# A hybrid decoder layer on one core: stores moved from SP to GpSimd, small copies to ScalarE, other token tiles, and fewer columns in two kinds of row

## The chip, the core and the metric

The kernel runs on one core of a Trainium2 chip. The core has TensorE (PE; its weight loads are shown apart as PEld), VectorE (DVE), ScalarE (ACT), GpSimd (POOL), the DMA queue of SyncE (SP), and 16 DMA engines that all queues share. Each engine takes its instructions in the order of its own list; semaphores tie the lists together. The metric is the device time of one execution in microseconds (us); less is better.

## What is computed

One layer of a decoder over 16 meta tokens, 1024 prompt tokens and 8 samples of 8 tokens (1104 tokens of width 1024). The reference, cut to what matters:

```
hn = rmsnorm(h, norm_mix_pre)
proj = hn @ w_in                      # 1024 -> 512 + 512 + 512 + 1024 + 1536 + 16
gate_b, gate_c, hv, z, xbc, dt_raw = split(proj)
u = gate_c * hv
conv_u, new_buf_sc = causal_dwconv(u, buf_sc, sconv_w)          # 3 taps
ya = group_rmsnorm(gate_b * conv_u, sconv_norm, 8)
xbc_c = silu(causal_dwconv(xbc, buf_xbc, ssm_conv_w) + ssm_conv_b)   # 4 taps
y, s = ssd_chunked(x, dt, A, B, C, s0)     # 16 meta tokens, 8 chunks of 128; samples from their own state
y = (y + D_skip * x) * silu(z)
yb = group_rmsnorm(y, ssm_norm, 2)
h = h + rmsnorm(concat(ya, yb) @ w_out, norm_mix_post)
fn = rmsnorm(h, norm_ffn_pre)
h = h + rmsnorm((silu(fn @ w_gate) * (fn @ w_up)) @ w_down, norm_ffn_post)
```

Returned are the outputs of the prompt and the samples (not of the meta tokens) and the new states: the last 2 rows of u, the last 3 rows of xbc, and the SSD state s.

## The kernel before

**Layout.** Channels lie on the partitions and tokens along the free dimension: a "row" is 128 channels of one projection by all 1104 tokens, in one of 5 buffers (`row_tile`). A row's tokens are in this order: 16 meta, 1024 prompt, 64 sample tokens. The tokens of one projection are cut into three tiles (`CUTS`): 272, 384 and 448 columns. The normalized input stands in SBUF once for each tile as a high and a low part (`xh`, `xl`); the weights of a row are split in the same way (`split_w`: a load `raw`, a copy `whi` on ACT, a subtraction `wlo` on DVE). `project_tile` makes one tile of one row: 8 blocks of the contraction by 3 products (high by high, low by high, high by low), 24 matmuls into one PSUM bank.

**Stages.** (1) Token tiles of x are loaded, normalized, transposed by PE (`split_x`) and split into `xh` and `xl`, while the first two xbc rows (8 and 9) and dt are projected. (2) The other xbc rows are projected, convolved (`taps`) and stored in DRAM (`d_xbc`). (3) The SSD's stretch: a loop over 8 chunks of 128 tokens (`ssd_chunk`, `y_of`), with the state updates of the samples (`sample_state`, 8 units) and the gating of finished chunks (`finish`) between. PE is filled there with the projections of z (`z_rows`, 8 rows) and of the short convolution (`sconv_gate` for c, `sconv_conv` for hv, called v, `sconv_out` for b, 4 rows each). (4) The output projection (`o`), (5) gate and up, (6) down.

**What passes through DRAM in stage 3.** `d_z` (z rows) and `d_y` (a chunk's y) are stored and loaded again by `finish`, as `zt` and `yf`; `finish` stores `d_yb`, and `sconv_out` stores `d_ya`, which stage 4 loads as `mrb` and `mra`. `sample_state` loads a state `s` (one of 2 buffers) and stores its successor to `o_nat`. A chunk loads its x, B and C (`xb`, 2 buffers), two tables of decays (`M`, 3 buffers; `E`, one), and has one buffer for y.

**Order.** The source gives instructions and priorities; a scheduler sets each engine's list when the program is built, from its own estimate of when operands and buffers are ready. A DMA stands in the list of the engine that issues it, here SP for all, and waits there until its data is ready or its buffer is free; what is behind it in that list waits too. Every DMA also waits until an earlier DMA that used its semaphore has landed; the semaphores of a queue are taken in turn, eight for SP and eight for GpSimd.

`sconv_conv` works like this: GpSimd clears the first 2 columns of u and copies the samples' history (`shist`) into u; the product of c and hv is written behind them, tile by tile; GpSimd copies u's last columns to `slast`, which leaves as the new state; ACT makes the last tap and DVE adds the others.

Of the kernel before, what the change touches and what calls it, by code (L numbers as in the profile page):

```python
# [27 lines left out]
DFF = 2816  # L28
NF = DFF // P
EPS = 1e-6  # L30
CUTS = [(0, 272), (272, 384), (656, 448)]
NT = 448
TT = [(0, NMETA)] + [(NMETA + P * i, P) for i in range(NCH)] + [(TS0, NS * LS)]
O_GB, O_GC, O_HV, O_Z, O_X, O_DT = 0, 512, 1024, 1536, 2560, 4096
ROW = 1152
HPF = 500
NACC = 2
YB = 1
SAMP = {1: (0,), 2: (1,), 3: (2, 3), 4: (4, 5), 5: (6,), 6: (7,)}
LATE = (9,)  # L40
WIDE = True
# [14 lines left out]
def hymba_kernel(ctx, tc, x_prompt, x_sample, state_sconv, state_ssm_conv, state_ssm, meta_tokens,  # L56
# [167 lines left out]
        for t in range(3):  # L224
            yield (t,) + project_tile(w_, t, name, skip=skip)

    def parts(t, pad):


        a, n = CUTS[t]  # L230
        b = a + n
        out = [(slice(0, min(b, TS0) - a), slice(pad + a, pad + min(b, TS0)))]
        if b > TS0:
            out.append((slice(TS0 - a, n), None))
        return out
# [65 lines left out]
    def split_x(i):  # L301

        xt, w = xts[i], P if i else MS
        pt = ps.tile([P, KD, P], F32, tag="big", name=f"xT{i}")
        for ks in (range(0, 4), range(4, 8)) if i < 3 else (range(KD),):
            for k in ks:
                PE.transpose(pt[:, k, :w], xt[:w, k * P:(k + 1) * P], ident[:w, :w])
            kk = slice(ks[0], ks[-1] + 1)
            for t0, c0, n in ((TT[i][0], 0, P),) if i else ((0, 0, NMETA), (TS0, NMETA, NS * LS)):
                t = max(q for q in range(3) if CUTS[q][0] <= t0)  # L310
                sl = slice(t0 - CUTS[t][0], t0 - CUTS[t][0] + n)
                dh, dl = xh[t][:, kk, sl], xl[t][:, kk, sl]
                S.activation(dh, pt[:, kk, c0:c0 + n], AF.Copy)
                V.tensor_tensor(out=dl, in0=pt[:, kk, c0:c0 + n], in1=dh.bitcast(F32), op=ALU.subtract)
# [205 lines left out]
    def y_of(i, xb, bt, xd, off):  # L520

        t0, w = TT[i]
        c = i - 1
        smp = i > NCH
        if smp:
            E = po.tile([P, 8, NS * LS], F32, tag="ES", name="ES")
            y = po.tile([P, 8, NS * LS], F32, tag="yS", name="yS")
        else:
            E = po.tile([P, 8, P], F32, tag="E", name=f"E{i}")
            y = po.tile([P, 8, P], F32, tag="y", name=f"y{i}", bufs=YB)  # L530
        for e in range(2):
            SY.dma_start(E[64 * e:64 * e + 64, :, :w],
                         d_e[:, c, :w].rearrange("(j e) t -> e j t", e=2)[e].partition_broadcast(64))
        pcb = ps.tile([P, 2, P], F32, tag="small", name=f"pcb{i}", bufs=NSM)
        cb = po.tile([P, 2, P], F32, tag="cb", name=f"cb{i}")
        mask = U if w == P else Us
        for g in range(2):
            PE.matmul(pcb[:w, g, :w], xb[:, 8 + g, :w], xb[:, 10 + g, :w], start=True, stop=True)
        V.tensor_tensor(out=cb[:w, :, :w], in0=pcb[:w, :, :w], in1=mask[:w, :w].unsqueeze(1).to_broadcast([w, 2, w]),
                        op=ALU.mult)  # L540
        Ms = []
        for g in range(2):
            M = m_tile(f"M{i}{g}")
            SY.dma_start(M[:w, :, :w], d_a[8 * g:8 * g + 8, c, :w].partition_broadcast(w))
            mg = M[:w, :, :w]
            for h in range(8):
                a_s = a_tok[:w, i, 8 * g + h:8 * g + h + 1]
                if g == 0:
                    V.tensor_scalar(out=M[:w, h, :w], in0=M[:w, h, :w], scalar1=a_s, scalar2=0.0,
                                    op0=ALU.subtract, op1=ALU.min)  # L550
                else:
                    S.activation(M[:w, h, :w], M[:w, h, :w], AF.Relu, scale=-1.0, bias=a_s)
            S.activation(mg, mg, AF.Exp, scale=1.0 if g == 0 else -1.0)
            V.tensor_tensor(out=mg, in0=mg, in1=cb[:w, g, :w].unsqueeze(1).to_broadcast([w, 8, w]), op=ALU.mult)
            Ms.append(M)
        if not smp:
            po_ = big(f"po{i}")
            pov = po_.rearrange("p (j t) -> p j t", j=8)
            off(pov)
        for j in range(8):  # L560
            S.activation(y[:, j, :w], xb[:, j, :w], AF.Copy, scale=Dp[:, j:j + 1])
        if not smp:
            V.tensor_tensor(out=E, in0=pov, in1=E, op=ALU.mult)
        pd_ = big(f"pd{i}")
        pdv = pd_.rearrange("p (j t) -> p j t", j=8)
        for h in range(H):
            e = h % 2
            PE.matmul(pdv[64 * e:64 * e + 64, h // 2, :w], xd[:w, h * 64:(h + 1) * 64], Ms[h // 8][:w, h % 8, :w],  # L568
                      start=True, stop=True)
        if not smp:  # L570
            V.tensor_tensor(out=y, in0=y, in1=E, op=ALU.add)
        V.tensor_tensor(out=y[:, :, :w], in0=pdv[:, :, :w], in1=y[:, :, :w], op=ALU.add)
        if smp:
            return E, y
        SY.dma_start(d_y[i][:, :, :], y)

    def finish(i):
        t0, w = TT[i]
        y = pf.tile([P, 8, P], F32, tag="yf", name=f"yf{i}", bufs=2)
        SY.dma_start(y[:, :, :w], d_y[i][:, :, :])  # L580
        zt = pf.tile([P, 8, P], F32, tag="zt", name=f"zt{i}")
        SY.dma_start(zt[:, :, :w], d_z[:, :, t0:t0 + w].rearrange("j p t -> p j t"))
        yv = y[:, :, :w]
        V.tensor_tensor(out=yv, in0=yv, in1=zt[:, :, :w], op=ALU.mult)
        sq = zt
        S.activation(sq[:, :, :w], yv, AF.Square)
        sg = pf.tile([P, 2, P], F32, tag="sg", name=f"sg{i}")
        sv = sq[:, :, :].rearrange("p (g j) t -> p g j t", g=2)[:, :, :, :w]
        V.tensor_tensor(out=sv[:, :, 0:2], in0=sv[:, :, 0:2], in1=sv[:, :, 2:4], op=ALU.add)
        V.tensor_tensor(out=sg[:, :, :w], in0=sv[:, :, 0], in1=sv[:, :, 1], op=ALU.add)  # L590
        pn = ps.tile([P, 2, P], F32, tag="small", name=f"pn{i}", bufs=NSM)
        PE.matmul(pn[:, :, :w], ones, sg[:, :, :w], start=True, stop=True)
        S.activation(sg[:, :, :w], pn[:, :, :w], AF.Sqrt, bias=eps_c, scale=0.25 / 512)
        V.reciprocal(sg[:, :, :w], sg[:, :, :w])
        for g in range(2):
            yg = y[:, 4 * g:4 * g + 4, :w]
            V.tensor_tensor(out=yg, in0=yg, in1=sg[:, g, :w].unsqueeze(1).to_broadcast([P, 4, w]), op=ALU.mult)
        SY.dma_start(d_yb[i][:, :, :], yv)

    def states(i, bt, xw):  # L600
        t0, w = TT[i]
# [15 lines left out]
    def z_rows():  # L617
        for j in range(8):
            row = row_tile(f"z{j}")
            for t, sl, pt in project(O_Z + j * P, f"pz{j}", NMETA):  # L620
                with tc.high_priority(offset=HPF):
                    S.activation(row[:, sl], pt, AF.Tanh, scale=0.5)
                    V.scalar_tensor_tensor(out=row[:, sl], in0=row[:, sl], scalar=1.0, in1=pt,  # L623
                                           op0=ALU.add, op1=ALU.mult)
            SY.dma_start(d_z[j][:, NMETA:T], row[:, NMETA:T])
            yield

    srow = {}

    def sconv_gate(j):  # L630
        gc = srow["gc", j] = row_tile(f"gc{j}")
        for t, sl, pt in project(O_GC + j * P, f"pc{j}"):
            with tc.high_priority(offset=HPF):
                S.activation(gc[:, sl], pt, AF.Copy)

    def sconv_conv(j):
        gc, u = srow["gc", j], row_tile(f"u{j}")
        smp = sample_rows(u, 2)
        G.memset(u[:, 0:2], 0.0)
        G.tensor_copy(smp[:, :, 0:2], shist[:, j, :].rearrange("p (b i) -> p b i", i=2))  # L640
        for t, sl, pt in project(O_HV + j * P, f"ph{j}"):
            for pc, rc in parts(t, 2):
                g_ = gc[:, sl.start + pc.start:sl.start + pc.stop]
                with tc.high_priority(offset=HPF):
                    if rc is not None:
                        V.tensor_tensor(out=u[:, rc], in0=pt[:, pc], in1=g_, op=ALU.mult)
                    else:
                        V.tensor_tensor(out=smp[:, :, 2:2 + LS], in0=b_i(pt[:, pc]), in1=b_i(g_), op=ALU.mult)
        G.tensor_copy(slast[:, j, 0:16].rearrange("p (b i) -> p b i", i=2), smp[:, :, LS:LS + 2])
        G.tensor_copy(slast[:, j, 16:18], u[:, TS0:TS0 + 2])  # L650
        wcol = lambda i: 60 + i * 4 + j
        taps(gc, u, 2, wcol, None, vec)
        taps(b_i(gc[:, TS0:T]), smp, 2, wcol, None, vec, None, lambda t, i: t[:, :, i:i + LS])

    def sconv_out(j):
        gc = srow["gc", j]
        for t, sl, pt in project(O_GB + j * P, f"pb{j}", NMETA):
# [10 lines left out]
            for h in (slice(0, n // 2), slice(n // 2, n)) if j == 3 else (slice(0, n),):  # L668
                V.reciprocal(sq[:, h], sq[:, h])
            V.tensor_tensor(out=gc[:, sl], in0=gc[:, sl], in1=sq, op=ALU.mult)  # L670
        SY.dma_start(d_ya[j][:, NMETA:T], gc[:, NMETA:T])

    def sconv_rows():
        for step in SORD.split():
# [49 lines left out]
    def sample_state(u, st):  # L724
# [38 lines left out]
        V.tensor_tensor(out=s0, in0=pt.rearrange("p (j n) -> p j n", j=8), in1=s0, op=ALU.add)  # L763
        for q in range(2):
            rows = slice((j0 + q) * P, (j0 + q + 1) * P)
            SY.dma_start(o_nat[b0:b0 + 4, rows, :].rearrange("b q n -> q b n"), s0[:, 4 * q:4 * q + 4, :])
        pv = ps.tile([P, 8, 3, LS], F32, tag="small", name=f"so{u}", bufs=NSM)
        for q in range(8):
            for n in range(3):
# [5 lines left out]
        V.tensor_tensor(out=t, in0=t, in1=E[:, j0:j0 + 2, tl], op=ALU.mult)  # L775
        V.tensor_tensor(out=y[:, j0:j0 + 2, tl], in0=y[:, j0:j0 + 2, tl], in1=t, op=ALU.add)
        if u == NS - 1:
            SY.dma_start(d_y[NCH + 1][:, :, :], y)

    def conv_states():  # L780
        for q in range(2):
# [3 lines left out]
            o = s_tile(f"xlo{q}")[0:27, :, :].rearrange("p j t -> p (j t)")[:, 0:6 * P]  # L785
            V.tensor_copy(o, pt[0:27, 0:6 * P])
            sl = slice(q * 6 * P, (q + 1) * 6 * P)
            SY.dma_start(o_xc_s[0].flatten_outer_dims()[:, sl], o[0:24, :])
            SY.dma_start(o_xc_p[0, 0][:, sl], o[24:27, :])

    def final_state():
        pt = big("fsp")
# [662 lines left out]
```

## Time and profile before

| what | us |
|---|---|
| three runs | 1412.11, 1418.18, 1409.39 |
| their median | 1412.11 |
| the profiled execution | 1411.28 |
| its span, first to last instruction | 1409.6 |

The profile is of one execution. Its page gives busy times of the engines, the chain of work that ended last, and the costliest groups of instructions; other views give the waits of each engine, busy times by stretch, and instructions in order of time. A row such as "L219 PE MATMUL px<-xh,whi" names the line, the engine, the operation, the tile written and the tiles read. SPq is SP's DMA queue. A matmul's duration contains its way through the array, and matmuls overlap: what one costs is the distance from its start to the next one's.

### The profile page before, as it was taken

The numbers are of one execution on the slowest core, as the hardware profiler recorded it, in microseconds if no ns is written. First come the engines' busy times: TensorE is split into PE (matmuls) and PEld (weight loads), VectorE is DVE, ScalarE is ACT, GpSimd is POOL, SyncE is SP. The second block draws the span as 40 slices with busy tenths as digits, with TensorE's granted clock in tenths as the row PEclk, the third lists the DMA queues.
The fourth block names the chain that finished last, engine by engine and source line by source line (L and its number), as shares of the span: only waits on it lengthen the run. The fifth ranks groups of instructions, "written<-read, shape, count | busy, mean of one in ns | idle before, by whom it ended". The sixth has DMA issues, their size and how long they took to land.

```text
span 1409.6 us, 22023 instructions
## 1 busy us (share of the span) xinstructions
PE 1374.2 (97%) x8841; PEld 1248.3 (89%) x8841; DVE 974.4 (69%) x1333; ACT 586.3 (42%) x946; POOL 50.7 (4%) x110
## 2 busy tenths in 40 slices
PE   7999999999999999999999999999999999999997
PEld 5899998788888987887889999999999998888886
DVE  6645457787797988687489877666767666455565
ACT  6456344444354344566554232222322334344431
POOL 1100000000000100011010000000000000000010
PEclk9999999999999999999999999999999999999999
DMA  6135246776746448775445553445343469655553
GB/s 212 47 88 168 81 117 192 199 207 196 203 136 191 133 135 282 243 228 179 146 140 181 189 195 116 162 163 174 133 140 107 160 218 324 228 179 165 180 161 129
DMA packets 212543, 240.51 MB, mean 171 GB/s; under 512 B 33421, under 2 KB 161505, under 8 KB 212442
## 3 DMA queue, kind: packets, MB, share of 16 engines
q1 hardware_dynamic: 212442, 239.12, 53.1%
q8 instruction: 69, 1.13, 0.3%
q14 instruction: 32, 0.26, 0.1%
HBM read 170.29 MB, written 68.79 MB: 170 GB/s over the span
## 4 chain that ended last, share of the span: by engine, by line
PE 79%; DVE 9%; DMA 7%; ACT 3%; issue 2%; SPq 0%; POOL 0%; DVEq 0%; POOLq 0%; ACTq 0%
PE d L1388 13%; PE px L219 10%; PE o L1004 9%; PE yg L1045 7%; PE yu L1045 7%; PE pz L219 5%; PE zg L1045 4%; PE zu L1045 4%; PE xu L1045 4%; PE xg L1045 4%; PE pb L219 2%; DMA M<-d_a 2%; PE pc L219 2%; DMA zt<-d_z 1%; PE pd L568 1%
## 5 line engine op out<-in xcount | busy, mean ns | idle before, releaser
L219 PE MATMUL px<-xh,whi 128*128 128x384 f32 (+2 forms) x288 | 94.1, 335 | 0.0
L219 PE MATMUL px<-xh,wlo 128*128 128x384 f32 (+2 forms) x288 | 92.7, 330 | 0.0
L219 PE MATMUL px<-xl,whi 128*128 128x448 f32 (+2 forms) x288 | 92.4, 331 | 0.0
L97 DVE TENSOR_TENSOR wlo<-raw,whi 128x1024 fp32r<-128x1024 f32 x32 | 39.1, 1222 | 55.8 <-ACT whi L105 55.7
L996 DVE SCALAR_TENSOR_TENSOR wol<-wo,vec,woh 128x1024 fp32r<-128x1024 f32 x36 | 45.9, 1278 | 30.7 <-ACT woh L995 30.7
L219 PE MATMUL pz<-xh,whi 128*128 128x256 f32 (+2 forms) x192 | 65.3, 340 | 1.1 <-DVE z L623 1.1
L219 PE MATMUL pz<-xl,whi 128*128 128x256 f32 (+2 forms) x192 | 63.4, 330 | 0.0
L219 PE MATMUL pz<-xh,wlo 128*128 128x256 f32 (+2 forms) x192 | 63.2, 329 | 0.0
L995 ACT ACTIVATE woh<-wo,vec 128x1024 fp32r<-128x1024 f32 x36 | 41.4, 1149 | 51.1 <-PE o L1004 42.0
L219 PEld LDWEIGHTS px<-xh,whi 128*128 128x128 f32 x288 | 53.8, 190 | 2.3 <-issue 0.2
L219 PEld LDWEIGHTS px<-xl,whi 128*128 128x128 f32 x288 | 53.1, 188 | 1.9
L219 PEld LDWEIGHTS px<-xh,wlo 128*128 128x128 f32 x288 | 53.3, 188 | 1.6
L1388 PE MATMUL d<-wd,B01h 128*128 128x512 f32 x176 | 54.2, 389 | 0.0
L249 DVE SCALAR_TENSOR_TENSOR xa<-xr,vec,xa 128x1128 f32<-128x1128 f32 x36 | 50.1, 1391 | 0.7
L1004 PE MATMUL o<-wol,mhb 128*128 128x512 f32 x144 | 44.5, 396 | 3.0 <-DVE wol L996 3.0
L1388 PE MATMUL d<-wd,T3h 128*128 128x512 f32 x152 | 46.8, 389 | 0.0
L1388 PE MATMUL d<-wd,T2h 128*128 128x512 f32 x144 | 44.2, 389 | 0.0
L1388 PE MATMUL d<-wd,B11h 128*128 128x512 f32 x144 | 44.2, 389 | 0.0
L276 ACT ACTIVATE xr<-px 128x384 f32<-128x384 f32 (+1 forms) x36 | 16.0, 457 | 58.5 <-PE px L219 58.4
L1004 PE MATMUL o<-woh,mlb 128*128 128x512 f32 x128 | 40.0, 391 | 0.0
L219 PEld LDWEIGHTS pz<-xh,whi 128*128 128x128 f32 x192 | 36.1, 188 | 4.2 <-issue 1.6
L105 ACT ACTIVATE whi<-raw 128x1024 fp32r<-128x1024 f32 x32 | 33.8, 1055 | 14.2 <-PE ph L219 8.9
(692 smaller groups left out, 4087.3 us busy)
## 6 DMA issues: line engine op xcount, KB each, us to landing
wo<-in_w_out_dram SPq DMA_DIRECT2D x36, 512.0 KB, 3.9
raw<-in_w_in_dram SPq DMA_DIRECT2D x32, 512.0 KB, 5.2
wg<-in_w_gate_dram SPq DMA_DIRECT2D x11, 1024.0 KB, 7.1
wu<-in_w_up_dram SPq DMA_DIRECT2D x11, 1024.0 KB, 5.2
xr<-in_w_down_dram SPq DMA_DIRECT2D x11, 1024.0 KB, 5.4
d_t<-xr SPq DMA_DIRECT2D x11, 1024.0 KB
xt<-in_x_prompt_dram SPq DMA_DIRECT2D x16, 512.0 KB, 6.4
M<-d_a SPq DMA_DIRECT2D x16, 512.0 KB, 5.1
```

The costliest lines, as they stand in the source:

```text
L97: V.tensor_tensor(out=out, in0=a, in1=hi.bitcast(F32), op=ALU.subtract)
L105: S.activation(hi[:, :], raw[:, :], AF.Copy)
L219: PE.matmul(acc, (hi, lo, hi)[q][:, wk], (xh, xh, xl)[q][t][:, k, o:], start=n_ == 0, stop=n_ + 1 == len(order))
L249: V.scalar_tensor_tensor(out=dst, in0=part(row, i), scalar=wv[:, wcol(i):wcol(i) + 1], in1=dst, op0=ALU.mult, op1=ALU.add)
L276: S.activation(row[:, rc], pt[:, pc], AF.Copy)
L568: PE.matmul(pdv[64 * e:64 * e + 64, h // 2, :w], xd[:w, h * 64:(h + 1) * 64], Ms[h // 8][:w, h % 8, :w], start=True, stop=True)
L995: S.activation(hi, raw, AF.Copy, scale=nv)
L996: V.scalar_tensor_tensor(out=lo, in0=raw, scalar=nv, in1=hi[:, :].bitcast(F32), op0=ALU.mult, op1=ALU.subtract)
L1004: PE.matmul(accs[i][c], l[:, kb, :], r_[:, c * 512:(c + 1) * 512], start=n == 0 and q == 0, stop=n == 11 and q == len(steps) - 1)
L1045: PE.matmul(acc[:, c, 0:W1], w_[l][k], b[r_][:, k, c * W1:(c + 1) * W1], start=start and k == 0 and x == 0, stop=k == 3 and x == 2, skip_g ...
L1388: PE.matmul(accs[t], sx[x][:, tl], wx[y], start=st and x + y == 0, stop=en and x == 1, skip_group_check=n not in OPENS)
```

## The change

Three things change.

Stores. In stage 3 the stores of z rows, of y (chunks and samples), of `d_yb` (chunks), of `d_ya`, of the samples' states, and of the last xbc rows (`conv_states`) are issued by GpSimd. The small copies of `sconv_conv` go from GpSimd to ACT.

Tiles. `CUTS` becomes 272, 320 and 512 columns. Token tile 5 (columns 528 to 655) now lies half in the second and half in the third tile, so `split_x` copies it in two parts.

Columns. The rows c and hv leave out the first 12 of the 16 meta tokens (`SKIP`), since their ya is never used; the taps of the prompt start at the first prompt token, so they read u from meta token 14 on, and the clearing of u's first columns goes away.

```
-CUTS = [(0, 272), (272, 384), (656, 448)]
-NT = 448
+CUTS = [(0, 272), (272, 320), (592, 512)]
+NT = 512
+SKIP = NMETA - 4
...
-    def parts(t, pad):
+    def parts(t, pad, skip=0):
...
+        a += skip if t == 0 else 0
+        n = b - a
...
-            for t0, c0, n in ((TT[i][0], 0, P),) if i else ((0, 0, NMETA), (TS0, NMETA, NS * LS)):
+            cut = [(TT[i][0], 0, P)] if i != 5 else [(TT[5][0], 0, P // 2), (TT[5][0] + P // 2, P // 2, P // 2)]
+            for t0, c0, n in cut if i else ((0, 0, NMETA), (TS0, NMETA, NS * LS)):
...
-        SY.dma_start(d_y[i][:, :, :], y)
+        G.dma_start(d_y[i][:, :, :], y)
...
-        SY.dma_start(d_yb[i][:, :, :], yv)
+        (G if w == P else SY).dma_start(d_yb[i][:, :, :], yv)
...
-            SY.dma_start(d_z[j][:, NMETA:T], row[:, NMETA:T])
+            G.dma_start(d_z[j][:, NMETA:T], row[:, NMETA:T])
...
-        for t, sl, pt in project(O_GC + j * P, f"pc{j}"):
+        for t, sl, pt in project(O_GC + j * P, f"pc{j}", SKIP):
...
-        G.memset(u[:, 0:2], 0.0)
-        G.tensor_copy(smp[:, :, 0:2], shist[:, j, :].rearrange("p (b i) -> p b i", i=2))
-        for t, sl, pt in project(O_HV + j * P, f"ph{j}"):
-            for pc, rc in parts(t, 2):
+        S.activation(smp[:, :, 0:2], shist[:, j, :].rearrange("p (b i) -> p b i", i=2), AF.Copy)
+        for t, sl, pt in project(O_HV + j * P, f"ph{j}", SKIP):
+            for pc, rc in parts(t, 2, SKIP):
...
-        G.tensor_copy(slast[:, j, 0:16].rearrange("p (b i) -> p b i", i=2), smp[:, :, LS:LS + 2])
-        G.tensor_copy(slast[:, j, 16:18], u[:, TS0:TS0 + 2])
+        S.activation(slast[:, j, 0:16].rearrange("p (b i) -> p b i", i=2), smp[:, :, LS:LS + 2], AF.Copy)
+        S.activation(slast[:, j, 16:18], u[:, TS0:TS0 + 2], AF.Copy)
...
-        taps(gc, u, 2, wcol, None, vec)
+        taps(gc[:, NMETA:TS0], u, 2, wcol, None, vec, None, lambda t, i: t[:, NMETA + i:TS0 + i])
...
-        SY.dma_start(d_ya[j][:, NMETA:T], gc[:, NMETA:T])
+        G.dma_start(d_ya[j][:, NMETA:T], gc[:, NMETA:T])
...
-            SY.dma_start(o_nat[b0:b0 + 4, rows, :].rearrange("b q n -> q b n"), s0[:, 4 * q:4 * q + 4, :])
+            G.dma_start(o_nat[b0:b0 + 4, rows, :].rearrange("b q n -> q b n"), s0[:, 4 * q:4 * q + 4, :])
...
-            SY.dma_start(d_y[NCH + 1][:, :, :], y)
+            G.dma_start(d_y[NCH + 1][:, :, :], y)
...
-            SY.dma_start(o_xc_s[0].flatten_outer_dims()[:, sl], o[0:24, :])
-            SY.dma_start(o_xc_p[0, 0][:, sl], o[24:27, :])
+            G.dma_start(o_xc_s[0].flatten_outer_dims()[:, sl], o[0:24, :])
+            G.dma_start(o_xc_p[0, 0][:, sl], o[24:27, :])
```

The engines' lists, as built. SP in stage 3, at the loads of chunk 3, before (a number behind a name tells buffers of one name apart):

```order
L532 DMA E_2419<-d_e 64x8x128 x2
L575 DMA d_y_80<-y_2083 128x1024
L580 DMA yf_3423<-d_y_80 128x1024
L766 DMA out_dram<-s_2164 128x4x128 x2
L744 DMA s_2833<-in_state_ssm_dram 128x4x128 x2
L625 DMA d_z<-z_2309 128x1088
L494 DMA xb_3208<-d_xbc 128x4x128
L494 DMA xb_3208<-d_xbc 128x8x128
L101 DMA raw<-in_w_in_dram 128x8x128
L532 DMA E_2751<-d_e 64x8x128 x2
L544 DMA M_2772<-d_a 128x8x128
L544 DMA M_3238<-d_a 128x8x128
```

The same place of SP's list now:

```order
L536 DMA E_2421<-d_e 64x8x128 x2
L548 DMA M_2762<-d_a 128x8x128
L102 DMA raw<-in_w_in_dram 128x8x128
L584 DMA yf_3425<-d_y_80 128x1024
L747 DMA s_2835<-in_state_ssm_dram 128x4x128 x2
L498 DMA xb_3210<-d_xbc 128x4x128
L498 DMA xb_3210<-d_xbc 128x8x128
L548 DMA M_2774<-d_a 128x8x128
L548 DMA M_3240<-d_a 128x8x128
L102 DMA raw<-in_w_in_dram 128x8x128
L536 DMA E_2753<-d_e 64x8x128 x2
```

The stores of y, s and z are gone from between the loads, and the two M loads stand ahead of the weight and E loads.

GpSimd's list, which before held at this place only the copies of u, now begins stage 3 so:

```order
L629 DMA d_z<-z_2222 128x1088
L579 DMA d_y_80<-y_2085 128x1024
L769 DMA out_dram<-s_2166 128x4x128 x2
L629 DMA d_z<-z_2311 128x1088
L579 DMA d_y_81<-y_2422 128x1024
L769 DMA out_dram<-s_2498 128x4x128 x2
L629 DMA d_z<-z_2554 128x1088
```

The stores stand among one another, and a late y now holds the state store behind it.

ACT's list at the first v rows, before:

```order
L105 ACTIVATE whi<-raw 128x1024
L634 ACTIVATE gc_3439<-pc_0_3446 128x272
L751 ACTIVATE s0t_3379<-s0p_3370 128x1024
L593 ACT_TABLE_LOAD
L593 ACTIVATE sg_3429<-pn_3432,eps_c 128x256
L634 ACTIVATE gc_3439<-pc_1_3472 128x384
```

And now:

```order
L106 ACTIVATE whi<-raw 128x1024
L638 ACTIVATE gc_3441<-pc_0_3448 128x260
L643 ACTIVATE u_3526<-shist 128x8x2
L643 ACTIVATE u_3828<-shist 128x8x2
L754 ACTIVATE s0t_3381<-s0p_3372 128x1024
L638 ACTIVATE gc_3441<-pc_1_3474 128x320
```

The two copies into new u rows stand ahead of the sample state's copy and of the next PSUM eviction, and the tiles have their new widths.

## The prediction

> **What bounds the kernel now.** I read the page's first part, then the stretches of the program, then the chain of waits and the waits of TensorE and of the SP queue. The first fence holds the page's span and busy times, and of the stretches those from the end of the x rows to the output projection (start to end, length, then busy time and instructions of PE, PEld, DVE, ACT, POOL, then granted clock, DMA share, GB/s).
>
> ```profile
> span 1409.6 us, 22023 instructions
> PE 1374.2 (97%) x8841; PEld 1248.3 (89%) x8841; DVE 974.4 (69%) x1333; ACT 586.3 (42%) x946; POOL 50.7 (4%) x110
> ...
> 132.00:188.00 56.00, 56.00 (x334) 53.61 (x333) 26.25 (x20) 21.63 (x38) 2.07 (x16) 1.00 0.32 99
> 188.00:280.00 92.00, 90.40 (x622) 79.32 (x620) 64.15 (x100) 41.46 (x94) 0.33 (x2) 1.00 0.65 177
> 280.00:380.00 100.00, 96.07 (x707) 85.61 (x708) 80.53 (x113) 41.08 (x76) 0.48 (x4) 1.00 0.68 191
> 380.00:480.00 100.00, 99.15 (x657) 87.93 (x655) 85.90 (x112) 45.29 (x80) 3.22 (x6) 1.00 0.54 160
> 480.00:560.00 80.00, 76.35 (x454) 66.46 (x453) 70.78 (x84) 34.80 (x57) 5.79 (x6) 1.00 0.60 200
> ```
>
> TensorE bounds it: 1374.2 of 1409.6 us, at full granted clock. The change lies in the SSD's stretch (188 to 560 us) and in the projections. In that stretch PE is busy 90.40 + 96.07 + 99.15 + 76.35 = 361.97 of 372 us, so all that better waits can give there is 10.0 us. What PE waited for there, and what the SP queue waited for there (line, what ended the wait: us in total, times, longest):
>
> ```profile
> PE so L770 <- ACT s0t L749: 3.1, 2, 2.4
> PE pz L219 <- DVE z L623: 1.1, 1, 1.1
> PE s0p L747 <- DVE s L763: 1.0, 1, 1.0
> PE pb L219 <- DVE gc L659: 1.0, 1, 1.0
> ...
> SPq L766 <- DVE s L763: 33.7, 6, 9.9
> SPq L598 <- DVE yf L597: 29.6, 5, 8.9
> SPq L544 <- PE pd L568: 20.4, 10, 6.8
> SPq L625 <- DVE z L623: 15.8, 5, 7.7
> SPq L744 <- DMA out_dram<-s: 13.5, 8, 5.3
> SPq L778 <- DVE yS L776: 10.0, 1, 10.0
> SPq L575 <- DVE y L572: 5.4, 5, 2.4
> ```
>
> SP runs its list in order. Stores that the change takes off it (L766, L598, L625, L778, L575) held it 33.7 + 29.6 + 15.8 + 10.0 + 5.4 = 94.5 us, and each load behind them waited too. Yet no PE wait names a DMA: they name ACT and DVE. One place shows how a late load reaches PE all the same, here in order of time (start, us, engine):
>
> ```profile
> 267.24 1.85 SPq L544 DMA_DIRECT2D M<-d_a  x2
> ...
> 273.47 2.45 ACT L552 ACTIVATE M<-M,a_tok 128x128 f32<-128x128 f32 x8 [8.19 <-DMA M<-d_a]
> ...
> 276.92 2.44 ACT L561 ACTIVATE y<-xb,Dp 128x128 f32<-128x128 f32 x8
> ```
>
> ACT sat 8.19 us for two M loads, then did M and y, and the s0t copy that PE wanted (the 2.4 us above) came behind them.
>
> **The change part by part.** Tile widths first. These are rows of the chain (start, us, matmuls) and of the order of time, first and last of a run at one width:
>
> ```profile
> 131.36 48.53 PE px L219 x288
> 765.44 3.01 PE yu L1045 x24
> 1232.88 104.27 PE d L1388 x460
> ...
> 185.75 0.37 PE L219 MATMUL px<-xl,whi 128*128 128x448 f32 x1
> 187.41 0.37 PE L219 MATMUL px<-xh,wlo 128*128 128x448 f32 x1
> 191.41 0.34 PE L219 MATMUL pz<-xh,whi 128*128 128x384 f32 x1
> 192.45 0.33 PE L219 MATMUL pz<-xh,whi 128*128 128x384 f32 x1
> ```
>
> Start to start, 272 columns cost 3.01/24 = 125.4 ns and 512 cost 104.27/460 = 226.7 ns: a line of 0.422 ns a column. On it 384 should cost 172.7 and does cost 1.04/6 = 173.3. 448 should cost 199.7 and costs 1.66/8 = 207.5. So the 448 tile is about 7.5 ns dear, for a reason that I can't see. The x rows confirm it: 48.53/288 = 168.5 ns, three tiles 505.5 ns. The new set, 320 taken from the line, is 125.4 + 145.7 + 226.7 = 497.8 ns. There are 32 projected rows (12 x, 8 z, 12 of the short convolution) of 24 matmuls a tile, 768 such threes: 768 x 7.7 ns = 5.9 us, all on PE. One end is that; the other is a 320 that is as dear as 448 (7.5 ns), which leaves 0. Elsewhere in the trace 448 runs nearer the line (first and last of a run of nine):
>
> ```profile
> 50.84 0.36 PE L219 MATMUL px<-xh,whi 128*128 128x448 f32 x1
> 52.66 0.36 PE L219 MATMUL px<-xh,whi 128*128 128x448 f32 x1
> ```
>
> That is 1.82/9 = 202.2 ns, 2.5 ns dear. I take 5 us, nearer the long run of 288.
>
> The c and hv rows skip 12 columns: 8 rows x 24 matmuls x 12 x 0.422 ns = 1.0 us of PE, a sure gain. ACT and DVE lose some columns too, beside PE.
>
> Token tile 5 is cut in two, with two copies and two subtractions of half size:
>
> ```profile
> L313 ACT ACTIVATE xh<-xT x14: 224/597/1030, 9.2 to 45.4; 128x1024 fp32r<-128x1024 f32 x6, 128x512 fp32r<-128x512 f32 x4, 128x64 fp32r<-128x64 f32 x2, 128x256 fp32r<-128x256 f32 x2
> ...
> 31.29 1.56 PE L258 MATMUL dt<-xh,wd 128*32 128x384 f32 x8 [1.19 <-ACT xh L313]
> 36.70 1.28 DVE L298 SCALAR_TENSOR_TENSOR xt<-xt,xr8r,pre_bc 128x1024 f32<-128x1024 f32 x1
> 44.23 1.03 PE L307 MATMUL xT<-ident,xt 128*128 128x128 f32 x8
> ```
>
> Two halves cost ACT 2 x 0.597 instead of 1.03 us. PE waits for that copy at 31.29; it now needs the first half alone, 0.43 us sooner. Against it, tile 1 covers less: 64 columns x (48 + 16 matmuls) x 0.422 = 1.7 us less PE work before tile 2 needs token tile 8. But that tile is ready at 38.0 and is transposed at 44.23, with 6 us to spare. I take 0, ends -0.4 and +1.7.
>
> Of the small copies, 12 go to ACT and four memsets go away. Below, the old copy, ACT's price for one as small, and the d_z stores as SP issued them (duration min/median/max, first and last start):
>
> ```profile
> L650 POOL COPY slast<-u x4: 184/782/2517, 397.8 to 530.7; 128x2 f32<-128x2 f32 x4
> 188.40 0.22 ACT L278 ACTIVATE xr<-px 128x64 f32<-128x64 f32 x1
> L625 SPq DMA_DIRECT2D d_z<-z x8: 319/338/502, 202.0 to 346.0; - x8
> ```
>
> 12 x 0.22 = 2.6 us of ACT, which is busy 163 of the 372 us. The last rows are copied beside the tap that waits for the same u; but the two first copies of history stand ahead of PSUM evictions in ACT's list and wait there for the stores that free their rows. Those are d_z stores, not the last ones; the last went out at 346.0, and the first v row is done at 397.8 (the copy's first start), so they have mostly landed. Cost 0.3 us, ends 0 and 2.
>
> The stores: 49 DMAs leave SP, where one takes 0.33 us (d_z, d_y, d_yb, d_ya) or 0.44 us (state):
>
> ```profile
> L575 SPq DMA_DIRECT2D d_y<-y x8: 320/332/2117, 245.4 to 513.0; - x8
> L766 SPq DMA_DIRECT2D out_dram<-s x16: 378/444/1262, 252.3 to 458.0; - x16
> ```
>
> 33 x 0.33 + 16 x 0.44 = 18 us of SP's time is freed, and the 94.5 us of waits. On PE the gain is at most the 10.0 us of idle time, less what loads don't cause: the waits for z (1.1), gc (1.0) and s (1.0) are for DVE, which is 80 to 86% busy. Later loads still wait for buffers (L544 for pd, 20.4 us), which stays. On POOL the stores wait in one list and block nobody but each other; POOL is idle there. What one costs on POOL no row shows; the nearest is the copy above: 184 ns where DVE is quiet, 2517 at worst. So a store may start up to 2.3 us late. For a store itself that is covered, except where a load waits for it (L744, 13.5 us in 8 waits, for the state buffers). Best end -8 us, worst +19 (8 state loads x 2.3 us, all of it reaching PE). I take -3: three tenths of the idle time, since one of its larger pieces, the 2.4 us at s0t, is a late load's.
>
> In the Trainium skill, "DMA: Bandwidth & Descriptors", section "Issuing engines are not separate DMA queues", says that DMAs from several engines run on the same 16 DMA engines and that another issuer saves only the sequencer's time. By that the 18 us of SP is all, it is not on PE's path, and the sum would be -5.7 instead of -8.7 us; the 94.5 us that SP waits speak for more.
>
> Sum: -5 - 1.0 + 0 + 0.3 - 3 = -8.7 us against the profiled execution. That one lasts 1411.3 us (its span and 1.7 us around it), 0.8 below the median of 1412.1: 1411.3 - 8.7 = 1402.6, say 1403 us.
>
> **The rivals.** First, idle time goes almost whole: loads move up, M arrives early, and -8 of the 10.0 us comes; with -5.9 and -1.0 that is 1396.5. For it speaks the 94.5 us; against it that four PE waits out of the list end with DVE, and that a list set for earlier loads puts their users earlier too.
>
> Second, earlier loads bring nothing: PE's list is filled with z and short-convolution work up to the loads' users, and the wait turns up elsewhere. -5 - 1 + 0.3: 1405.6. If 320 is dear as well, 1410.
>
> Third, slower: the state stores. A state load on SP waits for the store of two units before, and all of SP's list waits behind it. If POOL starts each store 2.3 us late and nothing hides it, 8 x 2.3 = 18.4 less 5.7 makes 1424. It turns the sign from 0.7 us for each of the eight. For it: the copy of 2517 ns, and DVE's load. Against: POOL's store no longer stands behind loads, and 13.5 us in eight waits never stopped PE by name. The Trainium skill, "SBUF — State Buffer", on the shared port says that GpSimd can't write descriptors while a two-port VectorE instruction runs; the spread of 184 to 2517 ns agrees that POOL is held up there, though no run here shows a store from it.
>
> **How the numbers follow.** Forecast (some idle time goes) 0.46, first rival 0.2, second 0.24, third 0.1. The range: down to the first rival with its start 2 us better, 1394; up past the second and its dear 320 and the lower half of the third, 1415. That leaves out some 0.15. One per cent, about what a measurement here can tell from no change, is 14.1 us: faster means below 1398, which is most of the first rival and a little of the forecast, 0.2; slower means above 1426, the third with more than its price, 0.05; within it 0.75.
>
> **What would show it.** Right: the x rows' run at about 166 ns a matmul, 512 columns at 227 and 320 at 146; the idle time of PE between 188 us and the output projection down from 10.0 to some 7 us; SP's waits there cut by most of 94.5 us; the M loads ahead of ACT's need. Wrong: 320 at 152 ns; SP waiting for out_dram<-s by far more than 13.5 us; ACT waiting for a store at u<-shist; or PE idle by as much as now at other places. My forecast fails most easily at the -3, which no row fixes.

## The result and the profile after

The changed kernel takes 1428.4 us (median of 6 runs, 1424.9 to 1430.8); the kernel before took 1412.5 beside it. The ratio is 1.0102, 95% interval 1.0084 to 1.0119: one per cent slower. The forecast was 1403 us, with a range up to 1415.

The fence holds lines of the changed kernel's page, then its stretches (start to end, length, busy time and instructions of PE, PEld, DVE, ACT, POOL, then granted clock, DMA share, GB/s):

```profile
span 1428.8 us, 22052 instructions
PE 1377.2 (96%) x8841; PEld 1234.9 (86%) x8841; DVE 973.7 (68%) x1334; ACT 588.2 (41%) x959; POOL 69.3 (5%) x143
...
188.00:280.00 92.00, 89.47 (x625) 76.20 (x623) 65.03 (x101) 43.82 (x97) 5.31 (x10) 1.00 0.64 177
280.00:380.00 100.00, 90.35 (x659) 77.47 (x660) 68.71 (x98) 36.14 (x71) 10.91 (x16) 0.95 0.61 169
380.00:480.00 100.00, 96.70 (x606) 82.69 (x605) 80.04 (x111) 44.68 (x82) 6.12 (x10) 0.97 0.58 167
480.00:560.00 80.00, 68.33 (x467) 59.21 (x466) 69.57 (x80) 30.42 (x58) 7.18 (x13) 0.92 0.49 151
```

In the SSD's stretch PE is busy 89.47 + 90.35 + 96.70 + 68.33 = 344.85 of 372 us: 27.1 us idle, where it was 10.0. And a column that was 1.00 throughout now falls: the granted clock. These are the stretches around its falls:

```profile
63.30:66.70 3.40, 3.40 (x18) 3.40 (x17) 3.40 (x9) 2.49 (x3) 0.08 (x1) 0.50 0.67 173
...
305.60:315.90 10.30, 5.08 (x22) 4.99 (x23) 9.22 (x18) 7.57 (x15) 2.08 (x3) 0.50 0.14 40
...
401.20:408.00 6.80, 6.70 (x17) 4.56 (x18) 5.93 (x15) 6.77 (x16) 0.76 (x1) 0.50 0.17 68
...
548.00:561.60 13.60, 4.89 (x12) 3.82 (x13) 9.07 (x13) 4.08 (x6) 0.53 (x1) 0.50 0.82 270
```

The clock is halved for one, three, two and four times 3.4 us. What that costs is seen in the matmuls of 272 columns in the first of them (in order of time; first and last of a run):

```profile
63.52 0.43 PE L220 MATMUL px<-xh,wlo 128*128 128x272 f32 x1
...
66.24 0.43 PE L220 MATMUL px<-xh,wlo 128*128 128x272 f32 x1
```

Twelve starts in 2.72 us are 226.7 ns from one to the next, against 125.4 ns at full clock: 45% of such time is lost. PE was busy 3.40 + 5.08 + 6.70 + 4.89 = 20.1 us of it, so by this estimate 9.0 us are lost. The whole then adds up: 17.1 us more idle, 9.0 us of clock, and tiles and skipped columns that give about 6 us (below), together +20, where the spans differ by 1428.8 - 1409.6 = 19.2 us.

What PE waited for, and what the SP queue, ACT and DVE waited for in the changed kernel (line, what ended the wait: us in total, times, longest), then the same two waits for M in the kernel before:

```profile
PE o L1007 <- ACT mhb L954: 11.4, 1, 11.4
PE s0p L750 <- DVE s L766: 7.7, 1, 7.7
...
PE pz L220 <- DVE z L627: 2.1, 1, 2.1
...
SPq L747 <- DMA out_dram<-s: 77.0, 7, 18.1
...
ACT M L556 <- DMA M<-d_a: 49.9, 9, 13.4
...
DVE M L553 <- DMA M<-d_a: 33.6, 8, 10.8
```

```profile
ACT M L552 <- DMA M<-d_a: 28.4, 7, 8.2
DVE M L549 <- DMA M<-d_a: 24.1, 8, 4.0
```

The 94.5 us that SP stood for stores are gone, but 63.5 us have come back at one line: the state load waits for the store of two units before, 77.0 us instead of 13.5. The M loads, which were to come ahead of need, are waited for longer: ACT and DVE wait 83.5 us for them, 52.5 before. Neither sum is a price by itself. Of the runs below, `stores_only_pool` has 41.0 us of the SP wait and doesn't differ clearly from the kernel before, and `tiles_only` has 71.0 us of the M waits and is 0.3% faster. What counts is where such a wait stops PE.

The first large stop, at 303 us, followed through the queues (start, us, engine; idle time before and what ended it):

```profile
281.36 0.77 POOL L769 DMA_DIRECT2D out_dram<-s  x1 [14.28 <-DVE s L766]
284.44 0.76 POOL L769 DMA_DIRECT2D out_dram<-s  x1 [2.31 <-issue]
285.19 0.56 POOL L629 DMA_DIRECT2D d_z<-z  x1
...
283.83 0.38 SPq L102 DMA_DIRECT2D raw<-in_w_in_dram  x1
291.03 0.99 SPq L747 DMA_DIRECT2D s<-in_state_ssm_dram  x2
292.12 1.00 SPq L498 DMA_DIRECT2D xb<-d_xbc  x2
293.24 1.08 SPq L548 DMA_DIRECT2D M<-d_a  x1
294.42 3.70 SPq L536 DMA_DIRECT2D E<-d_e  x2
298.21 0.65 SPq L548 DMA_DIRECT2D M<-d_a  x1
...
306.57 1.66 DVE L553 TENSOR_SCALAR M<-M,a_tok 128x128 f32<-128x128 f32 x8 [10.85 <-DMA M<-d_a]
...
310.82 1.97 PE L750 MATMUL s0p<-ident,s 128*128 128x128 f32 x8 [7.68 <-DVE s L766]
```

GpSimd issues the first store of a pair at once. The second starts 3.08 us later, after 2.31 us for which the profile names nothing ("issue"); on SP it starts 0.44 us after the first. SP, which has issued nothing since 284.2, gets to the state loads at 291.0, then issues xb, the first M, E and, at 298.2, the second M behind them. DVE stands 10.85 us for M, by the order of the two loads the second; the state update comes behind it in DVE's list, and PE's next state transpose waits 7.7 us for it.

The second stop is ahead of the output projection (columns as above):

```profile
541.11 0.54 POOL L602 DMA_DIRECT2D d_yb<-yf  x1 [10.67 <-DVE yf L601]
...
546.06 0.32 SPq L584 DMA_DIRECT2D yf<-d_y  x1
...
547.65 16.26 SPq L947 DMA_DIRECT2D mrb<-d_yb  x5
...
555.60 1.06 ACT L954 ACTIVATE mhb<-mrb 128x1024 fp32r<-128x1024 f32 x1 [11.83 <-DMA mrb<-d_yb]
...
556.71 1.22 PE L1007 MATMUL o<-woh,mhb 128*128 128x512 f32 x2 [11.44 <-ACT mhb L954]
```

The SSD's chain is late by now; the chain of waits puts the step from this d_yb store to the yf load behind it at 4.9 us, the landing, and the mrb loads stand behind the yf load in SP's list, though the first rows that they read were stored at 383 us.

### The profile page after: what moved, and what is told of

Same layout as the page of the kernel before. It is cut to its first block, busy times and chain, and to the rows that moved or that the text cites. A ratio compares the mean times of both kernels' runs of the same rounds, so it can differ in the third digit from the quotient of the medians.

```text
span 1428.8 us, 22052 instructions
## 1 busy us (share of the span) xinstructions
PE 1377.2 (96%) x8841; PEld 1234.9 (86%) x8841; DVE 973.7 (68%) x1334; ACT 588.2 (41%) x959; POOL 69.3 (5%) x143
## 4 chain that ended last, share of the span: by engine, by line
PE 55%; DVE 3%; issue 3%; DMA 2%; ACT 1%; SPq 0%; POOL 0%; DVEq 0%; POOLq 0%; ACTq 0%
PE d L1391 14%; PE o L1007 9%; PE yg L1048 7%; PE yu L1048 7%; PE zg L1048 4%; PE zu L1048 4%; PE xg L1048 4%; PE xu L1048 4%; DMA mrb<-d_yb 1%; PE d1s L1402 1%; PE d5s L1402 1%; PE fT L928 1%; DMA d_a<-f 0%; DMA d_yb<-yf 0%; DVE sq L672 0%
## 5 line engine op out<-in xcount | busy, mean ns | idle before, releaser
L220 PE MATMUL px<-xh,whi 128*128 128x272 f32 (+2 forms) x288 | 95.2, 339 | 0.0
L220 PE MATMUL px<-xl,whi 128*128 128x272 f32 (+2 forms) x288 | 93.7, 333 | 0.0
L220 PE MATMUL px<-xh,wlo 128*128 128x272 f32 (+2 forms) x288 | 93.4, 332 | 0.0
L1007 PE MATMUL o<-woh,mhb 128*128 128x512 f32 x144 | 40.0, 401 | 11.9 <-ACT mhb L954 11.4
L1007 PEld LDWEIGHTS o<-woh,mhb 128*128 128x128 f32 x144 | 26.7, 190 | 18.8 <-ACT mhb L954 11.7
L556 ACT ACTIVATE M<-M,a_tok 128x128 f32<-128x128 f32 (+1 forms) x72 | 21.7, 382 | 49.9 <-DMA M<-d_a 49.9
```

The costliest lines, as they stand in the source:

```text
L220: PE.matmul(acc, (hi, lo, hi)[q][:, wk], (xh, xh, xl)[q][t][:, k, o:], start=n_ == 0, stop=n_ + 1 == len(order))
L1007: PE.matmul(accs[i][c], l[:, kb, :], r_[:, c * 512:(c + 1) * 512], start=n == 0 and q == 0, stop=n == 11 and q == len(steps) - 1)
```

## The experiments

Sixteen kernels were run, in groups; each group's kernels ran beside runs of the kernel before on the same chip, so the ratio compares across groups (0.1% is 1.4 us). Theory names run on through the groups.

### Stores back, stores alone, halves of them

`stores_back_sp` undoes the move of all stores in the changed kernel, `stores_only_pool` makes that move alone in the kernel before, `state_back_sp` takes only the state stores back, and `state_only_pool` all others:

```diff
-            G.dma_start(o_nat[b0:b0 + 4, rows, :]...      # state_back_sp: this line alone
+            SY.dma_start(o_nat[b0:b0 + 4, rows, :]...
```

> The changed kernel with all seven kinds of store back on SP; tiles, skip, tile-5 split and ScalarE copies stay. Theory A (stores on GpSimd cost the time): the stall of the SSD's stretch falls back to about that of before (10 us), tiles and skip give their 7 us, so 1403 to 1408 us. Rival B (the new tiles set another order of work, and the order stalls): stays at 1422 to 1430 with PE idle still about 27 us between 188 and 560 us.

> The kernel before with nothing but the seven kinds of store on GpSimd. Theory A: slower by about 25 us, 1430 to 1440, with the stop of the second store of a state pair (about 3.1 us from one to the next, 0.44 on SP) in the trace. Rival B: 1405 to 1415, since tiles and order are those of before.

> The changed kernel with only the 16 state stores back on SP. Theory A1 (the state pairs on GpSimd delay SP's state loads, and with them all that stands behind them): nearly all comes back, 1403 to 1410, and SP's wait for out_dram<-s is under 20 us (77 in the changed kernel). Theory A2 (the y, yb, z and ya stores on GpSimd delay the end of the chain): 1420 to 1430, the stop before the output projection stays near 11 us.

> The changed kernel with only the 16 state stores on GpSimd, all others back on SP. Theory A1: 1420 to 1430, SP waits for out_dram<-s as in the changed kernel, about 70 us. Theory A2: 1403 to 1410.

| run | stores on GpSimd | median us | before | ratio (95%) |
|---|---|---|---|---|
| changed kernel | all | 1428.4 | 1412.5 | 1.0102 (1.0084 to 1.0119) |
| stores_back_sp | none | 1409.2 | 1412.7 | 0.9973 (0.9960 to 0.9986) |
| stores_only_pool | all, old tiles | 1414.3 | 1412.7 | 1.0011 (0.9998 to 1.0025) |
| state_back_sp | all but state | 1415.3 | 1412.7 | 1.0005 (0.9989 to 1.0021) |
| state_only_pool | state | 1416.8 | 1412.7 | 1.0026 (1.0009 to 1.0042) |

In the first run theory A has the cause right and its range by 1 us too low: PE's idle time in the stretch is back at 12.4 us, and with the stores on SP the kernel is a little faster than before, so in the changed kernel they cost 1428.4 - 1409.2 = 19 us. Theory A misses the second run widely (1430 to 1440 expected, rival B's range holds): in the kernel before, the same stores on GpSimd cost next to nothing, though the second store of a pair starts 3.0 to 5.5 us behind the first there too. A1 and A2 were put as alternatives, and neither holds: each half costs 6 to 8 us against `stores_back_sp`, both together 19. A1's wait is half there: SP stands 37.0 us for out_dram<-s in `state_only_pool`, not 70.

One pair of these runs is cleaner than the others. The scheduler makes new lists when stores move, and TensorE's rows stand in another order in most of these kernels. But the lists of TensorE, VectorE and ScalarE are row for row the same in `stores_back_sp` and `state_only_pool`. There the state pair costs 7.5 us. SP's list isn't quite the same: beside the stores, at two units a weight load (`raw`) stands ahead of the state loads in the second and behind them in the first; the runs with the loads on GpSimd (below) are without this difference. SP's rows of the first kernel, then SP's and GpSimd's of the second, at the same unit, and GpSimd's at the next:

```profile
275.10 0.94 SPq L769 DMA_DIRECT2D out_dram<-s  x2
...
278.88 0.93 SPq L747 DMA_DIRECT2D s<-in_state_ssm_dram  x2
```

```profile
281.76 0.38 SPq L102 DMA_DIRECT2D raw<-in_w_in_dram  x1
287.57 0.93 SPq L747 DMA_DIRECT2D s<-in_state_ssm_dram  x2
```

```profile
279.27 0.76 POOL L769 DMA_DIRECT2D out_dram<-s  x1 [26.00 <-DVE s L766]
282.38 0.75 POOL L769 DMA_DIRECT2D out_dram<-s  x1 [2.35 <-issue]
307.49 0.76 POOL L769 DMA_DIRECT2D out_dram<-s  x1 [24.36 <-DVE s L766]
312.91 0.75 POOL L769 DMA_DIRECT2D out_dram<-s  x1 [4.66 <-issue]
```

From the first store to the next load it was 3.8 us and is 8.3: 3.1 for the second store to start, and a longer landing. The first store of 279.27 landed after 2.8 us, that of 307.49 after 5.1, and both times the second started 0.30 us later. So it is in all 48 pairs of the six kernels here that have both whole stores of a pair on GpSimd: 0.30 to 0.37 us from the first's landing to the second's start.

Of the 9.5 us between the two spans (1417.6 and 1408.1) 3.2 are idle time of PE and by the estimate above 4.0 the clock, which fell for five steps of 3.4 us against two. One of the five came at 63.3 us, before any of these stores. Over all twelve runs of each the granted clock is 0.993 and 0.995, by estimate some 3 of the 7.5 us.

### Which part of the change the stores need to be dear

`old_tiles` is the changed kernel with the tiles of before, `copies_back_pool` with the small copies back on GpSimd, `tiles_only` the kernel before with the new tiles, and `split_state_pair` the changed kernel with one store of each pair on SP:

```diff
-            G.dma_start(o_nat[b0:b0 + 4, rows, :]...
+            (SY if q else G).dma_start(o_nat[b0:b0 + 4, rows, :]...
```

> The changed kernel with the old tile widths (272, 384, 448) and token tile 5 whole; stores, ScalarE copies and skip stay. Theory C (the stores cost little by themselves, 1.6 us in their run alone; they cost much where the new tiles' order leaves no slack at two places): 1412 to 1416 us, and neither the stop at about 303 us nor the one ahead of the output projection is over 4 us. Rival D (it is the stores with the skip or the copies): 1424 to 1432, with both stops.

> The changed kernel with the history and last-row copies back on GpSimd. Theory C: no help, 1424 to 1432, since the stores and the tiles are still together; perhaps more, as the copies then stand in GpSimd's list among the stores. Rival E (the copies on ScalarE hold the chain up): 1410 to 1418.

> The kernel before with nothing but the new tile widths and the cut of token tile 5. By the matmul spacings measured in the changed kernel (272: 125, 320: 147, 512: 227 ns) TensorE has 768 x 7 ns = 5.4 us less work. Theory F (the stretch of the SSD is held by its own chain, so the gain there turns into waiting): the x rows end about 2.5 us earlier and the whole is 1408 to 1411. Rival G (TensorE bounds throughout): 1406 to 1407.

> The changed kernel with one store of each state pair on GpSimd and the other on SP. Theory H (the second store of a pair on GpSimd starts only when the first has landed, 3.1 us on, and so every state load on SP starts 3 us late): the state loads start about 4 us after the last update of the state (7 now, 4.3 in the kernel before), SP's wait for out_dram<-s falls from 77 to under 50 us, and the time comes near that of the run with both on SP, 1415 to 1419. Rival I (any store on GpSimd lands late, because its landing takes as long whatever is beside it): 1424 to 1430.

| run | median us | before | ratio (95%) |
|---|---|---|---|
| old_tiles | 1417.6 | 1413.5 | 1.0031 (1.0020 to 1.0041) |
| copies_back_pool | 1428.5 | 1413.5 | 1.0100 (1.0078 to 1.0122) |
| tiles_only | 1409.8 | 1413.5 | 0.9971 (0.9958 to 0.9984) |
| split_state_pair | 1415.0 | 1413.5 | 0.9999 (0.9983 to 1.0015) |

Theory C: with the old tiles the stores cost little, and no stop of TensorE in the stretch is over 2.9 us, though the time is 1.6 us over the range it gave; the copies play no part (rival E falls). The tiles alone are worth 0.29%, 4.1 us: F's range, but not its reason, since PE's idle time in the stretch (9.7 us) didn't grow. H holds: taking one store of each of the eight pairs off GpSimd brings the changed kernel from 1.0102 to 0.9999, as much as taking both off (1.0005, with the same lists of TensorE, VectorE and ScalarE as here, and of SP but for the state stores).

### Why the second store waits, and the other stores

`state_quarters` cuts each state store of the changed kernel into two; `z_ya_pool` and `y_yb_pool` leave on GpSimd only what they name and the convolution's states:

```diff
+            for h in range(2):
+                G.dma_start(o_nat[b0 + 2 * h:b0 + 2 * h + 2, rows, :]..., s0[:, 4 * q + 2 * h:4 * q + 2 * h + 2, :])
```

> The changed kernel with each state store cut into two of two samples, so four of 128 KB on GpSimd for each unit instead of two of 256 KB. Theory J (GpSimd holds a store back while too many pieces of 512 bytes are under way: 512 of one store fit, 1024 don't): the second of the four starts about 0.6 us behind the first, and one of the later two starts only when an earlier one has landed. Rival K (a store of this shape waits for the last one of its kind, whatever its size): each of the four starts about 2.5 us or more behind the one before it, over 7 us in all. Time: 1424 to 1432 by J, over 1434 by K.

> The changed kernel with only the z and ya rows and the convolution's states stored by GpSimd, the state, y and yb stores on SP. Theory L (a store costs on GpSimd where a load or a buffer's next use soon waits for its landing, as for y, which has one buffer; z and ya are read much later): 1406 to 1410, as with all on SP or better, since SP's list is shorter. Rival M (the z stores held the z rows: TensorE waited 2.3 us for z at about 246 us): 1412 to 1416.

> The changed kernel with only the y and yb stores and the convolution's states stored by GpSimd, the state, z and ya stores on SP. Theory L: 1412 to 1416, as with the state alone back on SP. Rival M: 1407 to 1410.

GpSimd's rows in `state_quarters` in order of time, and what the state stores need to land there (ns, then us; shortest, median, longest):

```profile
279.01 2.16 POOL L770 DMA_DIRECT2D out_dram<-s  x3 [11.54 <-DVE s L766]
281.57 0.72 POOL L770 DMA_DIRECT2D out_dram<-s  x1 [0.40 <-issue]
282.29 0.56 POOL L629 DMA_DIRECT2D d_z<-z  x1
```

```profile
L770 POOL DMA_DIRECT2D out_dram<-s x32: 708/720/742, 252.6 to 484.0; - x32
...
DMA to landing us min/median/max: 2.0/2.2/5.8
```

Three stores go out back to back and the fourth starts 2.56 us after the first, which is the first's landing (2.2) and some 0.3 more. So it is in all eight units. A store here is 128 partitions by 2 samples, by its shape 256 pieces of 512 bytes. So 768 pieces may be under way and 1,024 not; two whole stores are 1,024, and a pair waits. Theory J holds in this, K falls. The limit isn't one of bytes: in the changed kernel the d_z store, 544 KB in 128 rows, follows the second state store at once (285.19 us), with 256 KB still under way. That it counts these pieces is inferred from the shapes; the profile's own packets on GpSimd's queue are larger (1,280 for the 16 stores of `state_only_pool`). It isn't the wait of a semaphore: the pair's second store has none but for a DMA eight earlier on this queue. The time is 1430.9 us, ratio 1.0114 (1.0092 to 1.0137): the last piece of a unit starts little sooner than before.

`z_ya_pool` gives 1413.4 us, 0.9997 (0.9984 to 1.0009), `y_yb_pool` 1415.7, 1.0011 (0.9996 to 1.0025). The second fits L's range and the first M's, so neither theory holds in both: z and ya too cost 0.24% against `stores_back_sp`. TensorE's lists of these two differ from that run's, so how much is landing and how much is order stays open.

### Through SP's list, or through the state?

`state_loads_pool` is `stores_back_sp` with the state loads on GpSimd, `tiles_state_loads_pool` the same in `tiles_only`, and `state_both_pool` the same in `state_only_pool`, so that SP no longer stands for a state store:

```diff
-            SY.dma_start(s0[:, 4 * q:4 * q + 4, :], s_nat...
+            G.dma_start(s0[:, 4 * q:4 * q + 4, :], s_nat...
```

> All stores on SP as in the run with the stores back, and the 16 state loads on GpSimd, so that SP no longer stands for a state store to land (12.9 us in that run). Theory N (the loss runs through SP's list: what stands behind the state load, above all the loads of M, comes late): 1403 to 1407, below both kernels. Theory O (it is the state itself that is late, not the list): 1408 to 1414, as the load pair on GpSimd is spaced by some 3 us as the stores were.

> The kernel before with the new tile widths and the 16 state loads on GpSimd; skip and ScalarE copies left away. Theory N: 1403 to 1408, 2 to 4 us under the run with the tiles alone. Theory O: 1409 to 1414.

> The changed kernel with the state stores and the state loads on GpSimd and all other stores on SP: the stores land as late as in the run with only the state stores on GpSimd (1416.8), the loads behind them later still, but SP's list holds none of it. Theory N: 1404 to 1411, and the M loads are issued as early as in the run with all stores on SP. Theory O: 1416 to 1424.

| run | median us | before | ratio (95%) |
|---|---|---|---|
| state_loads_pool | 1409.4 | 1415.2 | 0.9963 (0.9948 to 0.9979) |
| tiles_state_loads_pool | 1412.4 | 1415.2 | 0.9982 (0.9970 to 0.9995) |
| state_both_pool | 1416.4 | 1415.2 | 1.0010 (0.9997 to 1.0023) |

Each overlaps the run that it is made from (0.9973, 0.9971, 1.0026). So theory N falls: taking SP's wait away gave nothing back, though the queues look as if the 7.5 us went through it. O's ranges hold in all three, but its reason doesn't: in `state_loads_pool` the second loads of the pairs were issued some 5 us later and it cost nothing. In `state_both_pool` the loads stand behind the stores in GpSimd's queue and are later still, so it can't part the two ways. What the profile shows at 303 us agrees: in the changed kernel the M loads waited also for the matmuls that read their buffers, which ended between 289.6 and 290.6, little before SP was free at 291.0. Two waits ended close together there, and the one that the profile names was not the only one that bound. Which link carries the loss is not settled.

`state_loads_pool` and `state_both_pool` make another clean pair: but for the 16 state stores, all four lists, SP's too, are the same. The stores on GpSimd cost 1416.4 - 1409.4 = 7.0 us there, so the loss doesn't need the other order of the weight loads.

### One store of the pair, all else the same

> All stores on SP but the first of each state pair, which GpSimd stores. TensorE, VectorE and ScalarE run the same list as in the runs with all stores on SP and with both state stores on GpSimd, so only the landing differs. Theory P (what the state pair costs on GpSimd, 0.5% or 7.5 us between those two runs, is the wait of its second store for the first to land): ratio to the kernel before 0.9965 to 0.9985, as with all on SP. Rival Q (each state store on GpSimd costs half of it): 0.9995 to 1.001.

> The same with the second of each state pair on GpSimd and the first on SP, the list of the engines the same again. Theory P: 0.9965 to 0.9985, since nothing large stands ahead of the store in GpSimd's queue. Rival Q: 0.9995 to 1.001.

`first_state_pool` and `second_state_pool` are `stores_back_sp` with the first or the second store of each pair on GpSimd; the three engines' lists are again the same as in that run, and SP's state loads stand ahead of the weight loads as there. They give 1409.6 us, 0.9975 (0.9961 to 0.9990), and 1409.4, 0.9968 (0.9957 to 0.9980), with 1413.7 for the kernel before. In the second:

```profile
276.58 0.76 POOL L769 DMA_DIRECT2D out_dram<-s  x1 [27.28 <-DVE s L766]
...
280.37 0.93 SPq L747 DMA_DIRECT2D s<-in_state_ssm_dram  x2
```

The loads follow 3.8 us after the store, as on SP. Theory P holds and Q falls: a single state store on GpSimd, first or second, is free. The loss comes with two of them behind one another, and what sets these apart in the traces is the second store's wait for the first to land.

## Why the prediction was wrong

**The stores: the term that failed.** The prediction took -3 us from a range of -8 to +19, because SP stood 94.5 us for the moved stores and a late M had stopped PE once. Measured, the stores are +19 us in the changed kernel: the far end. The third rival, given 0.1, had the place right (SP's state load waits for the store of two units before) and came to 1424. Its cause was another: it let DVE hold up GpSimd's issue, from a copy of 2517 ns. No state store took longer than 786 ns, though DVE was busy 68.71 of 100 us there, and the first of a pair started at once (within 0.5 us of the state's update). The 3.1 us a unit came from the second store. That the far end, eight times 2.3 us, meets the measured 19 is luck: the step that it prices didn't occur. The argument against the rival, that 13.5 us in eight waits had never stopped PE by name, spoke of a kernel whose pair went out 0.44 us apart.

```profile
L769 POOL DMA_DIRECT2D out_dram<-s x16: 750/764/786, 252.5 to 480.0; - x16
```

The Trainium skill, "SBUF — State Buffer", section "SBUF: two separate sides", says that GpSimd can't write descriptors while a two-port VectorE instruction runs; stores of 750 to 786 ns show no such hold, though the rows don't tell which VectorE instructions are two-port. And by "DMA: Bandwidth & Descriptors", section "Issuing engines are not separate DMA queues", another issuer could gain no more than the sequencer's time. The measurement sides with that against the forecast's gain, and goes further, to a loss.

**The clock: a term that was not there.** "At full granted clock" was true of the kernel before and was taken as given. By the estimate above 9.0 of the 19.2 us between the spans are lost to it: 7.5 after stops of PE and 1.5 at 63.3 us, where PE hadn't stopped. A stop of 7.7 or 11.4 us costs its own length and 2 us more; at 401 us two short waits (1.7 and 0.5 us) were enough. The Trainium skill, "TensorE: Matmul & The Clock Gate", Part 1, says that the clock is halved after an idle window of some 3.4 us and restored after a busy one, and that the windows run on by themselves; the 3.4 us steps and the factor of two agree. A wholly idle step wasn't needed here: PE was busy 0.9, 1.3 and 0.7 us of the 3.4 us ahead of three of the falls, and throughout ahead of the first.

**The tiles.** Predicted -5 us, measured -4.1 (0.9971 of 1413.5, interval -5.9 to -2.3). In the changed kernel 512 columns cost what the line said and 320 one nanosecond more (first and last of a run, in order of time):

```profile
67.95 0.31 PE L220 MATMUL px<-xh,whi 128*128 128x320 f32 x1
...
69.71 0.31 PE L220 MATMUL px<-xh,whi 128*128 128x320 f32 x1
...
57.31 0.39 PE L220 MATMUL px<-xl,whi 128*128 128x512 f32 x1
...
60.03 0.39 PE L220 MATMUL px<-xl,whi 128*128 128x512 f32 x1
```

1.76/12 = 146.7 ns for 320 and 2.72/12 = 226.7 for 512; with 125.4 for 272 a three costs 498.8 instead of 505.5 ns, and 768 of them 5.1 us less.

**Skip, tile 5 and copies.** Forecast -0.7 us together; `stores_back_sp` has them and `tiles_only` doesn't (but for tile 5), and the two don't differ (0.9973 and 0.9971). Right as far as a run can tell.

**The idle time.** Forecast 10 down to 7 us, measured 27.1. The two signs named for being wrong, SP's wait for out_dram<-s far over 13.5 us and PE idle at other places, are both there.

**Readings.** Three of the prediction's readings are loose, and none moves its sum. DVE was busy 70 to 88% in the four stretches, not 80 to 86. Of the four PE waits that it shows, three end with DVE. And the copy of 184 ns isn't bound to a quiet DVE: the one at 530.66 us took as long beside a VectorE row of 1.28 us.

**What stays open.** By which link the late pair reaches PE isn't settled. With the lists of `stores_back_sp` the pair's wait costs 7.5 us; in the changed kernel removing it gives 14 us (1.0102 to 0.9999), but there the lists change too. Why the same pairs cost next to nothing with the old tiles is put down to the order of the lists; no run holds that order fixed. Nor do the runs split what the y, yb, z and ya stores cost, 3 to 6 us, into later landings and other lists.

No run is clearly better than `tiles_only`: the lowest ratio, 0.9963 of `state_loads_pool`, overlaps its 0.9971.

## What to carry to other kernels

A store moved to another queue doesn't only free the old queue: measure how far apart two of its kind start there and when they land, and follow who loads or reuses the buffer next. That a queue waits long for stores isn't a gain that can be booked; the work behind it may be bound by a buffer that comes free at the same moment. And where TensorE is near full, price an added stop of some microseconds with its clock penalty.

## What was not expected of the hardware

- GpSimd's queue took 768 pieces of 512 bytes at once, not 1,024 (pieces by the stores' shapes); the next store started 0.30 to 0.37 us after the first had landed. SP took pairs 0.44 us apart.
- The clock fell at 63.3 us without any stop of PE: it followed 2.17 us of matmuls of 16 columns (the line below). The same row stands in every kernel here, and in the kernel before the clock stayed at 1.00 there. With steps of 3.41 us counted from the clock's first change, 2.10 us or more of the row lay within one step in the ten traces in which it fell, and at most 2.04 in the eight in which it didn't. So the place of the steps decides, which differs from trace to trace, and a fall costs some 1.5 us (3.4 us at 45%).

```profile
60.34 2.17 PE L426 MATMUL pd<-I,dtT 32*128 32x16 f32 x18
```
